# Two block inversions shared by columns between VectorE and GpSimd, with masks, roots, loads and value products placed anew

## The chip, the cores and the metric

The kernel runs on one core of a Trainium2 chip. The metric is the device time of one execution in microseconds. Before the change it was 1900.02 us, the median of three runs (1899.34 to 1905.55).

## What is computed

One step of a small hybrid network, with a model width of 1024, on 640 tokens: 128 of context and 512 of a latent grid with 64 columns and 8 rows. Layer 0 mixes tokens with a gated DeltaNet in both directions (8 heads of 128), layer 1 with attention over a neighbourhood of the grid and over all context keys (16 heads of 64). Each is followed by a gated feed-forward layer with a convolution of width 3. Cut to what matters here, for one direction of one head of the DeltaNet:

```
a_mat = jnp.where(strict, jnp.einsum('nbhid,nbhjd->nbhij', kb, kc) * decay, 0.0)
t_mat = lax.linalg.triangular_solve(eye + a_mat, eye, left_side=True, lower=True)
u = jnp.einsum('nbhij,nbhjd->nbhid', t_mat, vc * bc[..., None])
w = jnp.einsum('nbhij,nbhjd->nbhid', t_mat, kb * jnp.exp(gc)[..., None])
...
def step(s, inp):
    v_new = ui - jnp.einsum('bhcd,bhde->bhce', wi, s)
    o = (jnp.einsum('bhcd,bhde->bhce', qi * jnp.exp(gi)[..., None], s)
         + jnp.einsum('bhcj,bhje->bhce', intra, v_new))
    s = (s * jnp.exp(g_last)[..., None, None]
         + jnp.einsum('bhcd,bhce->bhde', ki * jnp.exp(g_last[..., None] - gi)[..., None], v_new))
...
o = rmsnorm(o, norm_g) * jax.nn.silu(z.reshape(B, T, GDN_HEADS, GDN_DV))
```

`decay` is the exponential of a masked difference of cumulated gates. The triangular solve is the inverse of a unit triangular matrix per chunk. In layer 1 the part that the change touches is the sum over values, over the neighbourhood and over the context:

```
return (jnp.einsum('bhqrk,brkhd->bqhd', p_loc, v_blk)
        + jnp.einsum('bhqc,bchd->bqhd', p_ctx, v_ctx))
```

## The kernel before, in words

Activations lie with the width on the partitions and the tokens as columns. A projection (`prod`, L385 to L387) is made of three products of parts, high by high, low by high and high by low; `weights` loads each weight tile and splits it on ACT (L373) and on VectorE or GpSimd (L375). The stages follow each other in the trace: the start to about 60 us, the eight DeltaNet heads to about 550, the output projection, the feed-forward layer 0 to about 1050, attention from about 1100 to 1395, the feed-forward layer 1 to the end.

The heads' stage is a list of steps, `SCHED` (L573), of which each is a letter and a head: k, q, v and z are projections with convolution, K (`decay` and `keys`) makes the decay mask `dec` and the matrix `M` with its transpose `MT`, and stores its 32 x 32 diagonal blocks (`md`) from SyncE's queue. I (`invert`) inverts the diagonal blocks of two heads at once, so there are four inversions, I0 to I3. M (`merge`) builds the inverse of each head's whole chunks from the inverted blocks by matmuls of 32 and 64 columns (L848 and behind). Q and V make query products and scaled values, S (`scan`) runs the recurrence in five steps a direction, F (`finish`) the norm and the gate, a is a part of the next layers' modulation. A scheduler orders each engine's instructions statically from the steps' priorities (`PR`: S 2000, M 500, K 200, I 100, the others none) and from their dependences. At run time each engine, and each DMA queue, takes its instructions in that order.

An inversion works on 80 lanes (2 heads, 4 blocks, 2 directions, 5 chunks), each a 32 x 32 block in one partition. `lN` is loaded by SyncE's queue (L806); 31 steps of a multiplication into `lP` (L813) and an addition into `lY` (L819) run on GpSimd; then `lY` is stored (`yd`, L820), transposed by a copy into `lN` (L821) and stored (`wd`, L822), both from GpSimd's queue. Each of the three tiles has one buffer, so that an inversion begins when the one before it has let go of them.

`merge` fetches the blocks: `W6` and `Wx` are the tiles of factors, `M` takes the diagonal blocks beside its other ones. The loads of `M` (L834, L835) stand ahead of those of `W6` and `Wx` (L836 to L841). The page writes W for W6. The first product, p1, is made of pieces of W6, Wx and M; copies on VectorE (L865 and behind) bring p2 back into `M`.

`decay` adds the columns on VectorE (L698), masks each direction with an `affine_select` on GpSimd (L703), and takes the exponential on ACT (L708). `finish` works out the scale `so` of the norm in five small operations of VectorE (L984 to L988) and a power on GpSimd (L989); VectorE then scales the outputs `osb` (L991) and PE transposes them (L994).

In attention, a block of 128 queries and a pair of heads takes six value matmuls: per head two over the neighbourhood (L1324) and one over the context (L1327). The two heads of a pair lie in two halves of the array's columns.

Of the kernel before, what the change touches and what calls it, by code (L numbers as in the profile page):

```python
# [13 lines left out]
F32R = mybir.dt.float32r  # L14
AF = mybir.ActivationFunctionType
# [19 lines left out]
PR = {"S": 2000, "I": 100, "M": 500, "K": 200}  # L35
# [544 lines left out]
class Gdn:  # L580
# [17 lines left out]
    def tokens(self):  # L598
# [4 lines left out]
        for t, sgn in ((self.UT, 1), (self.LT, -1)):  # L603
            nc.gpsimd.affine_select(
                out=t, in_=net.ones, pattern=[[sgn, 128]], compare_op=ALU.is_ge, fill=0.0, base=0,
                channel_multiplier=-sgn,
            )
        abT = self.gp.tile([128, W], F32, tag="kT", name="abT", bufs=4)
# [69 lines left out]
    def decay(self, h):  # L678


        nc = self.nc
        t = self.gp.tile([128, 2, NBLK, 128], F32, tag="dec", name=f"dec{h}", bufs=4)
        self.dec[h] = t
        ngc = self.ngc.rearrange("p b (d h) -> p d b h", d=2)[:, :, :, h]
        for n, (out, col, parts) in enumerate((
            (t[:, 0, 1:], ngc[:, 0, 1:], [(0, b) for b in range(1, NBLK)]),
            (t[:, 1, 1:], ngc[:, 1, 1:], [(1, b) for b in range(1, NBLK)]),
            (t[:, :, 0], ngc[:, :, 0], [(0, 0), (1, 0)]),
        )):
# [12 lines left out]
        for d, sgn in ((0, 1), (1, -1)):  # L702
            nc.gpsimd.affine_select(  # L703
                out=t[:, d], in_=t[:, d], pattern=[[0, NBLK], [sgn, 128]], compare_op=ALU.is_ge, fill=-1e30,
                base=0, channel_multiplier=-sgn,
            )
        f = t.rearrange("p d b i -> p (d b i)")
        nc.scalar.activation(f, f, AF.Exp)  # L708
# [90 lines left out]
    def invert(self, nh, md, yd, wd, name):  # L799
# [5 lines left out]
        P = self.gp.tile([128, 256], F32, tag="lP", name=f"lP{name}", bufs=1)  # L805
        nc.sync.dma_start(N[:L], md.rearrange("h q d b r c -> (h q d b) r c")[:L])  # L806
# [3 lines left out]
        for i in range(31, 0, -1):  # L810
            n = 32 - i
            pr = P[:L, : i * n].rearrange("p (j c) -> p j c", c=n)
            nc.gpsimd.tensor_tensor(  # L813
                pr,
                N[:L, :i, i : i + 1].to_broadcast([L, i, n]),
                Y[:L, i : i + 1, i:].to_broadcast([L, i, n]),
                ALU.mult,
            )
            nc.gpsimd.tensor_tensor(Y[:L, :i, i:], Y[:L, :i, i:], pr, ALU.add)  # L819
# [4 lines left out]
    def merge(self, h, yd, wd):  # L824
# [6 lines left out]
        v = lambda t, q, d: t[q, d].rearrange("b r c -> r b c")  # L831
        for q in range(4):
            s = slice(32 * q, 32 * q + 32)
            nc.sync.dma_start(M[s, 0, :, s], v(yd, q, 0))  # L834
            nc.sync.dma_start(M[s, 1, :, s], v(wd, q, 1))  # L835
        nc.sync.dma_start(W6[0:32, :, 0:32], v(wd, 0, 0))  # L836
        nc.sync.dma_start(W6[32:64, :, 32:64], v(wd, 1, 0))
        nc.sync.dma_start(W6[64:96, :, 0:32], v(yd, 2, 1))
        nc.sync.dma_start(W6[96:128, :, 32:64], v(yd, 3, 1))
        nc.sync.dma_start(Wx[64:96], v(wd, 2, 0))  # L840
        nc.sync.dma_start(Wx[32:64], v(yd, 1, 1))  # L841
# [134 lines left out]
    def finish(self, h):  # L976
# [4 lines left out]
        so = gp.tile([128, 4, NBLK], F32, tag="so", name=f"so{h}", bufs=2)  # L981
        for b in range(NBLK):
            nc.scalar.activation(sq[:, b], osb[:, b], AF.Square, accum_out=so[:, 0, b : b + 1])
        nc.vector.tensor_scalar(so[:, 1], ssq, 128.0, None, ALU.mult)  # L984
        nc.vector.reciprocal(so[:, 2], so[:, 1])
        nc.vector.tensor_tensor(so[:, 0], so[:, 0], so[:, 2], ALU.mult)
        nc.vector.tensor_scalar(so[:, 0], so[:, 0], 1.0 / 128, EPS, ALU.mult, ALU.add)
        nc.vector.tensor_tensor(so[:, 0], so[:, 0], so[:, 1], ALU.mult)  # L988
        nc.gpsimd.tensor_tensor(so[:, 3], so[:, 0], self.net.mhalf[:, :NBLK], ALU.pow)  # L989
# [33 lines left out]
    def run(self):  # L1023
# [4 lines left out]
        def step(op, h):  # L1028
# [14 lines left out]
            elif op == "I":  # L1043
                self.invert(2, *scr[h], h)
# [17 lines left out]
        for t in SCHED.split():  # L1062
            if t[0] in PR:
                with net.tc.high_priority(PR[t[0]]):
# [86 lines left out]
class Na:  # L1151
# [91 lines left out]
    def attend(self, p):  # L1243
# [51 lines left out]
        for cb in range(4):  # L1295
# [25 lines left out]
            for e in range(2):  # L1321
                out = O[H[e], cb * 128 : cb * 128 + 128]
                for j in range(2):
                    nc.tensor.matmul(  # L1324
                        out, vw[:n, cb, j, H[e]], pt[:n, 2 * e + j], start=(j == 0), stop=False, tile_position=(0, 64 * e)
                    )
                nc.tensor.matmul(  # L1327
                    out, self.cv[:, p * 128 + 64 * e : p * 128 + 64 * e + 64], pc[:, e], start=False, stop=True,
                    tile_position=(0, 64 * e),
                )  # L1330
# [313 lines left out]
```

## Time and profile before

| what | number |
|---|---|
| median of three runs | 1900.02 us |
| profiled execution | 1899.56 us |
| its span | 1897.9 us |
| granted clock of PE, mean | 0.977 |
| PEclk, 50 to 250 us and 350 to 400 us | 0.86 to 0.90 |
| inversions on GpSimd, first operation | 114.5, 188.1, 318.8, 431.9 us |

The profile is of one execution. Busy time is the time in which an engine ran an instruction; the span is from the first to the last. In lists of the trace a row has start, length, engine, line, operation, output and inputs, and in square brackets the idle time ahead of it and what ended it. A row of waits gives the total time, how often, and the longest. A line that a helper holds, such as L385, stands for many uses, told apart by the tiles' names, where numbers are left out.

### The profile page before, as it was taken

To read this page: it belongs to the slowest core of one execution; us is meant where nothing else is said; L and a number is where in the kernel's file an instruction comes from. 1 tells how busy PE (TensorE), PEld (TensorE's weight loads), DVE (VectorE), ACT (ScalarE), POOL (GpSimd) and SP (SyncE) were. 2 spreads that over 40 slices of the span, in tenths; PEclk is the share of its full clock that TensorE was granted. 3 is DMA by queue.
4 is the path that set the end of the run, shared out by engine and by line. 5 is a ranking of instruction groups with operands and counts; after the bars stand their busy time and mean duration, and the time that the engine had idled before them with its cause. 6 is when DMAs were issued, how large, how long until landed. Compare 5 with 4: busy or idle time off the path is not lost.

```text
span 1897.9 us, 34312 instructions
## 1 busy us (share of the span) xinstructions
PE 1794.2 (95%) x13587; PEld 1710.2 (90%) x13587; DVE 1207.2 (64%) x2876; ACT 725.2 (38%) x1458; POOL 345.5 (18%) x549
## 2 busy tenths in 40 slices
PE   6886699899999999999999999999999999999998
PEld 5885689799889999999999988888899999999998
DVE  6664467475567999755356699555678743553564
ACT  4444235254353331232234444444453421431443
POOL 1364703518002112100000211111131000000000
PEclk9897899899999999999999999999999999999999
DMA  7223133322242455442223254222233312222231
GB/s 294 73 83 84 36 114 107 92 79 81 63 150 69 161 173 159 140 156 62 87 86 104 76 163 154 78 70 69 69 123 119 121 53 77 87 71 76 88 91 56
DMA packets 102481, 194.16 MB, mean 102 GB/s; under 512 B 39496, under 2 KB 59034, under 8 KB 99560
## 3 DMA queue, kind: packets, MB, share of 16 engines
q1 hardware_dynamic: 93760, 162.88, 27.0%
q0 software_dynamic: 8016, 28.56, 4.7%
q8 instruction: 107, 1.75, 0.4%
q10 hardware_dynamic: 544, 0.52, 0.1%
q14 instruction: 54, 0.44, 0.1%
HBM read 183.09 MB, written 12.46 MB: 103 GB/s over the span
## 4 chain that ended last, share of the span: by engine, by line
PE 48%; DVE 5%; issue 2%; DMA 2%; ACT 1%; POOL 0%; DVEq 0%; POOLq 0%; ACTq 0%
PE duv L385 4%; PE duv L386 4%; PE duv L387 4%; PE dug L385 4%; PE dug L386 4%; PE dug L387 4%; PE rdn L385 4%; PE rdn L386 4%; PE rdn L387 4%; PE dvn L385 1%; DMA bias<-cols 1%; PE dvn L387 1%; PE dvn L386 1%; PE no L1324 1%; PE dqn L385 1%
## 5 line engine op out<-in xcount | busy, mean ns | idle before, releaser
L385 PE MATMUL duv<-hh,whuv 128*128 128x256 f32 (+1 forms) x704 | 217.6, 309 | 6.0 <-DVE yv L442 6.0
L385 PE MATMUL rdn<-F,whdn 128*128 128x384 f32 (+1 forms) x704 | 216.2, 307 | 2.5 <-DVE X L451 2.5
L387 PE MATMUL duv<-hh,wluv 128*128 128x256 f32 (+1 forms) x704 | 217.0, 308 | 0.4 <-DVE wluv L375 0.4
L386 PE MATMUL duv<-hl,whuv 128*128 128x256 f32 (+1 forms) x704 | 217.1, 308 | 0.0
L385 PE MATMUL dug<-hh,whug 128*128 128x256 f32 (+1 forms) x704 | 215.7, 306 | 1.0 <-DVE yg L442 1.0
L386 PE MATMUL dug<-hl,whug 128*128 128x256 f32 (+1 forms) x704 | 215.7, 306 | 0.0
L387 PE MATMUL dug<-hh,wlug 128*128 128x256 f32 (+1 forms) x704 | 215.7, 306 | 0.0
L386 PE MATMUL rdn<-F,whdn 128*128 128x384 f32 (+1 forms) x704 | 215.6, 306 | 0.0
L387 PE MATMUL rdn<-F,wldn 128*128 128x384 f32 (+1 forms) x704 | 215.5, 306 | 0.0
L385 PEld LDWEIGHTS duv<-hh,whuv 128*128 128x128 f32 x704 | 133.4, 189 | 6.6 <-ACT whug L373 3.8
L385 PEld LDWEIGHTS rdn<-F,whdn 128*128 128x128 f32 x704 | 132.4, 188 | 3.1 <-PE rdn L387 1.9
L387 PEld LDWEIGHTS duv<-hh,wluv 128*128 128x128 f32 x704 | 133.2, 189 | 0.8 <-DVE wluv L375 0.8
L385 PEld LDWEIGHTS dug<-hh,whug 128*128 128x128 f32 x704 | 132.5, 188 | 1.2 <-issue 1.2
L386 PEld LDWEIGHTS duv<-hl,whuv 128*128 128x128 f32 x704 | 133.2, 189 | 0.0
L386 PEld LDWEIGHTS rdn<-F,whdn 128*128 128x128 f32 x704 | 132.2, 188 | 0.0
L387 PEld LDWEIGHTS dug<-hh,wlug 128*128 128x128 f32 x704 | 132.2, 188 | 0.0
L387 PEld LDWEIGHTS rdn<-F,wldn 128*128 128x128 f32 x704 | 132.1, 188 | 0.0
L386 PEld LDWEIGHTS dug<-hl,whug 128*128 128x128 f32 x704 | 132.1, 188 | 0.0
L451 DVE SCALAR_TENSOR_TENSOR X<-rdn,mods,X 128x128 f32<-128x128 f32 (+1 forms) x144 | 54.9, 432 | 116.7 <-PE rdn L387 116.5
L373 ACT CAST whdn<-wstdn 128x896 fp32r<-128x896 f32 (+1 forms) x48 | 47.0, 979 | 211.5 <-PE rdn L386 120.9
L373 ACT CAST whug<-wstug 128x1024 fp32r<-128x1024 f32 x44 | 46.2, 1050 | 143.8 <-PE dug L386 120.4
L375 DVE TENSOR_TENSOR wldn<-wstdn,whdn 128x896 fp32r<-128x896 f32 (+1 forms) x48 | 54.3, 1132 | 58.9 <-ACT whdn L373 58.9
(704 smaller groups left out, 4823.7 us busy)
## 6 DMA issues: line engine op xcount, KB each, us to landing
wstuv<-w_up SPq DMA_DIRECT2D x44, 512.0 KB, 3.5
wstug<-w_up SPq DMA_DIRECT2D x44, 512.0 KB, 3.5
adat<-w_ada SPq DMA_DIRECT2D x20, 1024.0 KB, 6.7
adr<-w_adar POOLq DMA_DIRECT2D x80, 256.0 KB, 3.1
wstdn<-w_dn SPq DMA_DIRECT2D x32, 448.0 KB, 3.3
wstdn<-w_dn SPq DMA_DIRECT2D x16, 512.0 KB, 3.5
adr<-w_adar SPq DMA_DIRECT2D x32, 256.0 KB, 2.8
wstqT<-w_gin SPq DMA_DIRECT2D x8, 512.0 KB, 4.4
```

What stands on the lines that cost most here:

```text
L373: nc.scalar.copy(wh[:, c], st[:, c])
L375: ins = eng.tensor_tensor(wl[:, c], st[:, c], wh[:, c].bitcast(F32), ALU.subtract).ins
L385: nc.tensor.matmul(out, a, mh, start=first, stop=False)
L386: nc.tensor.matmul(out, a, ml, start=False, stop=False)
L387: ins = nc.tensor.matmul(out, b, mh, start=False, stop=last).ins
L451: nc.vector.scalar_tensor_tensor(x, ps[:, base + c0 : base + c1], self.mod(l, gi, m, v), x, ALU.mult, ALU.add)
L1324: nc.tensor.matmul(out, vw[:n, cb, j, H[e]], pt[:n, 2 * e + j], start=(j == 0), stop=False, tile_position=(0, 64 * e))
```

## The change

`invert` gets a column `cut`: columns from the cut on are worked by VectorE, those below it by GpSimd, with two parts of a wider `lP`. `CUT` is 24, 24, 32, 32, so that I0 and I1 give 8 of 32 columns to VectorE (62 operations; GpSimd keeps 46 of its 62), and I2 and I3 stay on GpSimd. I0's priority becomes 1000. The load of `lN` moves from SyncE's queue to GpSimd's. In `merge` four loads, two for W6 and two for Wx, stand first. The decay mask becomes an addition of a constant tile `far` (0 or -1e30), which GpSimd builds once; VectorE does the addition. The power in `finish` becomes an integer seed and three Newton steps on VectorE. The value matmuls alternate between the two heads.

```diff
-PR = {"S": 2000, "I": 100, "M": 500, "K": 200}
+CUT = (24, 24, 32, 32)
+PR = {"S": 2000, "I": 100, "I0": 1000, "M": 500, "K": 200}
...
+        self.far = self.gs.tile([128, 2, 128], F32, tag="far", name="far")
+        nc.gpsimd.memset(self.far, 0.0)
+        for d, sgn in ((0, 1), (1, -1)):
+            nc.gpsimd.affine_select(
+                out=self.far[:, d], in_=self.far[:, d], pattern=[[sgn, 128]], compare_op=ALU.is_ge, fill=-1e30,
+                base=0, channel_multiplier=-sgn,
+            )
...
-        for d, sgn in ((0, 1), (1, -1)):
-            nc.gpsimd.affine_select(
-                out=t[:, d], in_=t[:, d], pattern=[[0, NBLK], [sgn, 128]], compare_op=ALU.is_ge, fill=-1e30,
-                base=0, channel_multiplier=-sgn,
+        for d in range(2):
+            nc.vector.tensor_tensor(
+                t[:, d], t[:, d], self.far[:, d].unsqueeze(1).to_broadcast([128, NBLK, 128]), ALU.add
             )
...
-        P = self.gp.tile([128, 256], F32, tag="lP", name=f"lP{name}", bufs=1)
-        nc.sync.dma_start(N[:L], md.rearrange("h q d b r c -> (h q d b) r c")[:L])
+        P = self.gp.tile([128, 336], F32, tag="lP", name=f"lP{name}", bufs=1)
+        P = P[:, 144:], P
+        nc.gpsimd.dma_start(N[:L], md.rearrange("h q d b r c -> (h q d b) r c")[:L])
...
         for i in range(31, 0, -1):
-            n = 32 - i
-            pr = P[:L, : i * n].rearrange("p (j c) -> p j c", c=n)
-            nc.gpsimd.tensor_tensor(
-                pr,
-                N[:L, :i, i : i + 1].to_broadcast([L, i, n]),
-                Y[:L, i : i + 1, i:].to_broadcast([L, i, n]),
-                ALU.mult,
-            )
-            nc.gpsimd.tensor_tensor(Y[:L, :i, i:], Y[:L, :i, i:], pr, ALU.add)
+            for eng, p, lo, hi in ((nc.vector, P[0], max(i, cut), 32), (nc.gpsimd, P[1], i, cut)):
+                n = hi - lo
+                if n > 0:
+                    pr = p[:L, : i * n].rearrange("p (j c) -> p j c", c=n)
+                    eng.tensor_tensor(
+                        pr,
+                        N[:L, :i, i : i + 1].to_broadcast([L, i, n]),
+                        Y[:L, i : i + 1, lo:hi].to_broadcast([L, i, n]),
+                        ALU.mult,
+                    )
+                    eng.tensor_tensor(Y[:L, :i, lo:hi], Y[:L, :i, lo:hi], pr, ALU.add)
...
+        nc.sync.dma_start(W6[96:128, :, 32:64], v(yd, 3, 1))
+        nc.sync.dma_start(Wx[32:64], v(yd, 1, 1))
+        nc.sync.dma_start(W6[0:32, :, 0:32], v(wd, 0, 0))
+        nc.sync.dma_start(Wx[64:96], v(wd, 2, 0))
         for q in range(4):
...
-        nc.sync.dma_start(W6[0:32, :, 0:32], v(wd, 0, 0))
         nc.sync.dma_start(W6[32:64, :, 32:64], v(wd, 1, 0))
         nc.sync.dma_start(W6[64:96, :, 0:32], v(yd, 2, 1))
-        nc.sync.dma_start(W6[96:128, :, 32:64], v(yd, 3, 1))
-        nc.sync.dma_start(Wx[64:96], v(wd, 2, 0))
-        nc.sync.dma_start(Wx[32:64], v(yd, 1, 1))
...
-        nc.vector.tensor_scalar(so[:, 1], ssq, 128.0, None, ALU.mult)
-        nc.vector.reciprocal(so[:, 2], so[:, 1])
-        nc.vector.tensor_tensor(so[:, 0], so[:, 0], so[:, 2], ALU.mult)
-        nc.vector.tensor_scalar(so[:, 0], so[:, 0], 1.0 / 128, EPS, ALU.mult, ALU.add)
-        nc.vector.tensor_tensor(so[:, 0], so[:, 0], so[:, 1], ALU.mult)
-        nc.gpsimd.tensor_tensor(so[:, 3], so[:, 0], self.net.mhalf[:, :NBLK], ALU.pow)
+        V.tensor_scalar(so[:, 1], ssq, 128 * EPS, None, ALU.mult)
+        V.scalar_tensor_tensor(so[:, 0], so[:, 0], 1.0 / 128, so[:, 1], ALU.mult, ALU.add)
+        x, t, y = so[:, 0], so[:, 2], so[:, 3]
+        V.tensor_scalar(t.bitcast(I32), x.bitcast(I32), 1, None, ALU.logical_shift_right)
+        V.tensor_scalar(y.bitcast(I32), t.bitcast(I32), -1.0, float(0x5F3759DF), ALU.mult, ALU.add)
+        V.tensor_scalar(x, x, -0.5, None, ALU.mult)
+        for _ in range(3):
+            V.tensor_tensor(t, y, y, ALU.mult)
+            V.tensor_tensor(t, t, x, ALU.mult)
+            V.scalar_tensor_tensor(y, t, 1.5, y, ALU.add, ALU.mult)
...
-                self.invert(2, *scr[h], h)
+                self.invert(2, *scr[h], h, CUT[h])
...
-            for e in range(2):
-                out = O[H[e], cb * 128 : cb * 128 + 128]
-                for j in range(2):
+            for j in range(3):
+                for e in range(2):
```

The scheduler places the instructions anew. On GpSimd, in the middle of I0 (lP0, lN0 and lY0 are its tiles), stood head 3's two masks before; behind the additions stands the shape of a lane's part:

```order
L813 TENSOR_TENSOR lP0_1326<-lN0_1324,lY0_1325 80x231
L819 TENSOR_TENSOR lY0_1325<-lY0_1325,lP0_1326 80x11x21
L813 TENSOR_TENSOR lP0_1326<-lN0_1324,lY0_1325 80x220
L703 AFFINE_SELECT dec3_1244<-dec3_1244 128x640 x2
L819 TENSOR_TENSOR lY0_1325<-lY0_1325,lP0_1326 80x10x22
L813 TENSOR_TENSOR lP0_1326<-lN0_1324,lY0_1325 80x207
```

The same part of I0 on GpSimd now, with its smaller shapes:

```order
L831 TENSOR_TENSOR lY0_1317<-lY0_1317,lP0_1318 80x13x11
L825 TENSOR_TENSOR lP0_1318<-lN0_1316,lY0_1317 80x144
L831 TENSOR_TENSOR lY0_1317<-lY0_1317,lP0_1318 80x12x12
L781 TENSOR_TENSOR irk2_1053<-k2ss_1046,half_626 128x5
L825 TENSOR_TENSOR lP0_1318<-lN0_1316,lY0_1317 80x143
L831 TENSOR_TENSOR lY0_1317<-lY0_1317,lP0_1318 80x11x13
```

The masks dec3 are gone from the inversion, and so is the power of so0 from I1 further behind; the small operation irk2 of head 2's keys, which stood inside I0 before too, is still there.

On VectorE, at the copies that bring M0's product p2 back, the rows were these (dec0 and kq0s belong to head 0's queries, wlqT2 to a weight tile, vT2 to head 2's value projection):

```order
L898 TENSOR_TENSOR dec0_721<-kq0s_1425,dec0_721 128x512 x2
L375 TENSOR_TENSOR wlqT2_2533<-wstqT20_2530,whqT2_2532 128x1024
L865 COPY M0_780<-p20_1693 32x5x32 x4
L869 COPY W60_1652<-p30_1714 32x5x32 x2
L442 SCALAR_TENSOR_TENSOR vT2_1813<-dvT20_1763,sm_61,vT2_1813 128x127
L442 SCALAR_TENSOR_TENSOR vT2_1813<-dvT20_1763,sm_61,vT2_1813 128x254
```

Now the first nine operations of I1 (lP1, lN1, lY1) stand between the weight tile and M0's copies:

```order
L377 TENSOR_TENSOR wlqT2_2617<-wstqT20_2614,whqT2_2616 128x1024
L825 TENSOR_TENSOR lP1_1555<-lN1_1553,lY1_1554 80x31
L831 TENSOR_TENSOR lY1_1554<-lY1_1554,lP1_1555 80x31
L825 TENSOR_TENSOR lP1_1555<-lN1_1553,lY1_1554 80x60
L831 TENSOR_TENSOR lY1_1554<-lY1_1554,lP1_1555 80x30x2
L825 TENSOR_TENSOR lP1_1555<-lN1_1553,lY1_1554 80x87
L831 TENSOR_TENSOR lY1_1554<-lY1_1554,lP1_1555 80x29x3
L825 TENSOR_TENSOR lP1_1555<-lN1_1553,lY1_1554 80x112
L831 TENSOR_TENSOR lY1_1554<-lY1_1554,lP1_1555 80x28x4
L825 TENSOR_TENSOR lP1_1555<-lN1_1553,lY1_1554 80x135
L877 COPY M0_784<-p20_1777 32x5x32 x4
L881 COPY W60_1736<-p30_1798 32x5x32 x2
```

From there on operations of I1 stand singly between those of the scan S0 and of M0.

On PE, ahead of M0's first product p10, stood the last products of the second half of head 0's z projection (dzs01, from hh and hl, the two parts of the input):

```order
L385 MATMUL dzs01_2443<-hh_75,whzs0_2414 128x260
L386 MATMUL dzs01_2443<-hl_76,whzs0_2414 128x260
L742 MATMUL v0tp_1507<-ident_63,vT0_1492 128x128
L387 MATMUL dzs01_2443<-hh_75,wlzs0_2415 128x260
L848 MATMUL p10_1670<-W60_1652,M0_780 32x32
L848 MATMUL p10_1670<-Wx0_1653,M0_780 32x32 x2
```

Now 22 products of the first half of head 1's (dzs10) stand there, of which the last four are shown ahead of it, and p10 begins among them:

```order
L387 MATMUL dzs10_2561<-hh_75,whzs1_2557 128x384
L388 MATMUL dzs10_2561<-hl_76,whzs1_2557 128x384
L389 MATMUL dzs10_2561<-hh_75,wlzs1_2558 128x384
L387 MATMUL dzs10_2561<-hh_75,whzs1_2557 128x384
L860 MATMUL p10_1754<-W60_1736,M0_784 32x32
L388 MATMUL dzs10_2561<-hl_76,whzs1_2557 128x384
L389 MATMUL dzs10_2561<-hh_75,wlzs1_2558 128x384
```

So a part of one dense projection that came behind M0 stands ahead of it.

More of the change, by code (lines that the diff above doesn't have):

```diff
@@ L14 @@
 F32R = mybir.dt.float32r
+I32 = mybir.dt.int32
 AF = mybir.ActivationFunctionType
@@ L797, in keys, with invert @@
                 )
-    def invert(self, nh, md, yd, wd, name):
+    def invert(self, nh, md, yd, wd, name, cut=32):
         nc = self.nc
@@ L981, in finish @@
         so = gp.tile([128, 4, NBLK], F32, tag="so", name=f"so{h}", bufs=2)
+        V = nc.vector
         for b in range(NBLK):
             nc.scalar.activation(sq[:, b], osb[:, b], AF.Square, accum_out=so[:, 0, b : b + 1])
-        nc.vector.tensor_scalar(so[:, 1], ssq, 128.0, None, ALU.mult)
-        nc.vector.reciprocal(so[:, 2], so[:, 1])
-        nc.vector.tensor_tensor(so[:, 0], so[:, 0], so[:, 2], ALU.mult)
-        nc.vector.tensor_scalar(so[:, 0], so[:, 0], 1.0 / 128, EPS, ALU.mult, ALU.add)
-        nc.vector.tensor_tensor(so[:, 0], so[:, 0], so[:, 1], ALU.mult)
-        nc.gpsimd.tensor_tensor(so[:, 3], so[:, 0], self.net.mhalf[:, :NBLK], ALU.pow)
+        V.tensor_scalar(so[:, 1], ssq, 128 * EPS, None, ALU.mult)
[8 more added lines that the diff above has]
+            V.scalar_tensor_tensor(y, t, 1.5, y, ALU.add, ALU.mult)
         for b in range(NBLK):
@@ L1063, in run @@
             if t[0] in PR:
-                with net.tc.high_priority(PR[t[0]]):
+                with net.tc.high_priority(PR.get(t, PR[t[0]])):
                     step(t[0], int(t[1]))
@@ L1320, in attend @@
             yield
-            for e in range(2):
-                out = O[H[e], cb * 128 : cb * 128 + 128]
-                for j in range(2):
+            for j in range(3):
+                for e in range(2):
+                    if j < 2:
+                        v_, p_ = vw[:n, cb, j, H[e]], pt[:n, 2 * e + j]
+                    else:
+                        v_, p_ = self.cv[:, p * 128 + 64 * e : p * 128 + 64 * e + 64], pc[:, e]
                     nc.tensor.matmul(
-                        out, vw[:n, cb, j, H[e]], pt[:n, 2 * e + j], start=(j == 0), stop=False, tile_position=(0, 64 * e)
-                    )
[L1327 to L1330, printed above, removed]
+                        O[H[e], cb * 128 : cb * 128 + 128], v_, p_, start=(j == 0), stop=(j == 2),
+                        tile_position=(0, 64 * e),
+                    )
             ps = nxt
```

## The prediction

> **What bounds the kernel now.** The page comes first, for the engine that carries the span; then the waits of PE, for the places where PE stands still; then the waits of the other engines around the largest.
>
> ```profile
> span 1897.9 us, 34312 instructions
> PE 1794.2 (95%) x13587; PEld 1710.2 (90%) x13587; DVE 1207.2 (64%) x2876; ACT 725.2 (38%) x1458; POOL 345.5 (18%) x549
> ...
> PE kk3s L761 <- ACT k3ts L751: 16.7, 1, 16.7
> PE sb L925 <- ACT osb L957: 14.7, 1, 14.7
> ...
> PE p L848 <- DMA W<-wd: 9.4, 3, 5.1
> ...
> ACT dec L708 <- POOL dec L703: 16.9, 1, 16.9
> DVE osb L991 <- POOL so L989: 15.3, 1, 15.3
> ACT osb L957 <- DVE w L953: 19.0, 5, 15.7
> ```
>
> PE is busy 1794.2 of 1897.9 us, so 103.7 us of idle time is all that this change can win, apart from the values and from a slow clock. (The profiled execution took 1899.56 us: the span and 1.66 around it. The sum below is against it; it is 0.46 under the median.) The columns of the waits are total, times and longest. The two largest inside the work are single stalls, and the last three rows name their causes: ACT stood 16.9 us behind a decay mask that GpSimd had not done, and VectorE 15.3 us behind the power `so`. Both are GpSimd instructions, queued behind an inversion:
>
> ```profile
> 114.53 0.25 POOL L813 TENSOR_TENSOR lP<-lN,lY 80x31 f32<-80x31 f32 x1 [4.68 <-DMA lN<-md]
> 144.91 1.45 POOL L703 TENSOR_SCALAR_AFFINE_SELECT dec<-dec 128x640 f32<-128x640 f32 x2
> 156.75 0.25 POOL L819 TENSOR_TENSOR lY<-lY,lP 80x31 f32<-80x31 f32 x1
> ...
> 168.48 0.22 PE L848 MATMUL p<-W,M 32*32 32x32 f32 x2 [3.38 <-DMA W<-wd]
> 169.46 0.52 PE L848 MATMUL p<-Wx,M 32*32 32x32 f32 x3 [0.77 <-DMA Wx<-wd]
> ...
> 220.55 1.17 POOL L989 TENSOR_TENSOR so<-so,mhalf 128x5 f32<-128x5 f32 x1
> ```
>
> I0 runs from 114.53 to 157.0 with head 3's masks near its end, at 144.91. M0's first product comes at 168.48, 11.5 us after I0. So the 16.7 us stall and M0's 3.38 and 0.77 hang on one thing, I0's elapsed time: without the masks PE is at M0 earlier and waits there. The second stall ends with the power at 220.55, inside I1.
>
> **a) I0 in two halves, up to M0.** A GpSimd operation is priced by its smallest and largest shapes.
>
> ```profile
> 139.37 0.67 POOL L819 TENSOR_TENSOR lY<-lY,lP 80x252 f32<-80x252 f32 x1
> ...
> 118.20 1.21 DVE L375 TENSOR_TENSOR wlvT<-wstvT,whvT 128x1024 fp32r<-128x1024 f32 x1
> 119.34 0.43 DVE L780 TENSOR_SCALAR D<-D 128x5 f32<-128x5 f32 x1
> 119.69 0.15 DVE L781 TENSOR_TENSOR D<-D,edl 128x5 f32<-128x5 f32 x1
> 119.76 0.15 DVE L780 TENSOR_SCALAR D<-D 128x5 f32<-128x5 f32 x1
> L557 DVE TENSOR_TENSOR yv<-yv,yg 128x640 f32<-128x640 f32 x44 | 36.2, 823 | 25.4 <-ACT yg L556 25.4
> ```
>
> From 0.25 us (31 elements) to 0.67 (252) it is 1.9 ns an element over 0.19; the gap to the next is about 0.08. GpSimd keeps 46 of 62 operations and 4600 of 10,912 elements: 46 x 0.27 + 4600 x 0.0019 = 21.2, and 1.2 for the one power left among them (irk2, priced as the one of `so`): 22 us, done near 137. VectorE gets 62 operations, 6312 elements. It has no row of this shape; from 0.15 us (5), 0.82 (640) and 1.21 (1024) it is 1.04 ns an element, with starts 0.07 apart (119.69, 119.76): 62 x 0.07 + 6312 x 0.00104 = 10.9 us. These stand one by one among its other work:
>
> ```profile
> 109.00:157.00 48.00, 31.23 (x215) 29.85 (x213) 23.15 (x66) 17.68 (x36) 38.69 (x67) 0.82 0.23 67
> 180.00:201.00 21.00, 20.96 (x251) 18.55 (x249) 12.75 (x40) 8.60 (x33) 11.11 (x24) 1.00 0.42 132
> 201.00:225.00 24.00, 9.27 (x74) 8.17 (x73) 6.27 (x16) 6.65 (x25) 21.52 (x36) 0.77 0.08 28
> 225.00:240.00 15.00, 14.11 (x101) 13.20 (x100) 9.61 (x28) 4.72 (x11) 6.43 (x12) 0.92 0.30 69
> ```
>
> The columns are the window, its length, busy time of PE, PEld, DVE, ACT and POOL with counts, and the clock. DVE is busy 23.15 of the 48 us; some 21 of it falls behind 114.5. Packed, its half ends at 114.5 + 10.9 + 21 = 147 (an estimate). The other end comes from a contention that the rows show:
>
> ```profile
> 118.33 1.41 POOL L819 TENSOR_TENSOR lY<-lY,lP 80x135 f32<-80x135 f32 x1
> 153.38 0.46 POOL L819 TENSOR_TENSOR lY<-lY,lP 80x135 f32<-80x135 f32 x1
> ```
>
> The same add takes 0.46 us at 153.38 and 1.41 at 118.33, where VectorE's 128x1024 subtraction (118.20, 1.21 long) lies over it; and L780 behind that took 0.43 us instead of 0.15, until 119.77, as the add ended. So here either blocked the other for a whole operation. If no part of the split ran beside the other, and half of VectorE's other 21 us (taken as the part with two tiles of SBUF to read) did not either, the end is 114.5 + 22 + 10.9 + 10.5 = 158. I take the middle, 152.5: the blocking rows are those of long operations, and VectorE's half has short ones, but its queue also waits for PE.
>
> From I0's end to M0 lay 11.5 us. Of the loads that p1 (M0's first product) needs, some stood last:
>
> ```profile
> 160.44 0.55 POOL L822 DMA_DIRECT2D wd<-lN  x1 [0.31 <-POOL lN L821]
> ...
> 167.54 0.43 SPq L840 DMA_DIRECT2D Wx<-wd  x1
> ...
> lN<-md SPq DMA_DIRECT2D x4, 320.0 KB, 6.1
> ...
> wd<-lN POOLq DMA_DIRECT2D x4, 320.0 KB, 3.0
> ...
> 1112.83 0.34 PE L386 MATMUL dkn<-hl,whkn 128*128 128x384 f32 x1
> 1113.00 0.34 PE L387 MATMUL dkn<-hh,wlkn 128*128 128x384 f32 x1
> ```
>
> Wx's piece was issued at 167.54, after ten others; now it is among the first four, but it cannot start before `wd` has landed (issue 160.44, 3.0 us). Four issues of 0.43 to 0.5 us go from ahead of it: 1.9 us off, so 9.6. M0 is at 157 to 168, taken 162.1: -6.4. PE also does 22 products of head 1's z, 0.17 us apart (1112.83, 1113.00), 3.8 us, ahead of M0 that stood behind it; half of it I count as won, -2. **Together -8** (0 to -16: M0 at 168 with nothing won, or at 157 with all of it). PE itself could be at M0 at 168.5 - 3.4 - 16.7 + 3.8 = 152, so I0's end decides.
>
> **b) I1's VectorE half, among the scans.** In 180 to 201, S0 runs: PE is busy 20.96 of 21 us, so products fill the scan's waits, and DVE 12.75. An operation of I1's half is on average 0.15 + 6312/62 x 0.00104 = 0.26 us, 16 us for all; in DVE's 8.25 idle us they cost nothing, ahead of a scan operation all of it. I take a third exposed: +5 (0 to 16). Nine of them also stand ahead of M0's copies:
>
> ```profile
> 171.71 1.32 DVE L865 COPY M<-p 32x160 f32<-32x160 f32 x4 [5.26 <-PE p L848]
> ```
>
> They wait for lN's load, which is issued behind the `wd` store on GpSimd's queue: 160.44 - 157.0 + 0.3 and 3.0 us for the store, 6.1 for the load (3.0 if it lands like the store), 2.5 for the nine: 15.3 us after I0's end, or 12.2. The copies came 3.2 us behind M0's first product, so now 9.6 + 3.2 = 12.8 after I0. So +2 (0 to 2.5). **Together +7.**
>
> **c) The power gone from I1.** The 14.7 us stall goes: `so` is worked out on VectorE in 14 operations of 0.15 to 0.2 us, 2.5 us in place of a wait of 15.3. The clock stood at 0.92 for 14.11 busy us behind the stall: 1.1 more. **-16** (-10 if the merge M2 is next late: of the 9.4 us in three waits for W it has 0.9, beside 5.1 and 3.4).
>
> **d) M4, behind I2, which stays on GpSimd whole.**
>
> ```profile
> 318.78 0.25 POOL L813 TENSOR_TENSOR lP<-lN,lY 80x31 f32<-80x31 f32 x1 [2.63 <-DMA lN<-md]
> 356.82 1.11 POOL L819 TENSOR_TENSOR lY<-lY,lP 80x31 f32<-80x31 f32 x1
> 368.41 0.28 PE L848 MATMUL p<-W,M 32*32 32x32 f32 x2 [5.10 <-DMA W<-wd]
> ```
>
> PE waits 5.1 us there. Between head 5's key products and M4 the order has products that take 50 us at full clock before and 39 now (each at the spacing of its shape; an estimate), so PE is there 11 us earlier in the chain. The chain gets some 4.5 us shorter (1.9 for the reordered loads, up to 3.1 for a load that lands like a store on GpSimd's queue). 11 - 4.5, less 1.5 as the moved products fill gaps ahead of M2: **+5** (-2 with a tie between the two, +9 with a chain no shorter).
>
> **e) Attention values,** 32 blocks:
>
> ```profile
> 1113.27 0.71 PE L1324 MATMUL no<-ptw,vw 92*64 92x128 f32 x6
> 1113.76 0.28 PE L1327 MATMUL no<-ptc,cv 128*64 128x128 f32 x1
> 1113.81 0.27 PE L1324 MATMUL no<-ptw,vw 92*64 92x128 f32 x1
> 1114.03 0.38 PE L1327 MATMUL no<-ptc,cv 128*64 128x128 f32 x2
> ```
>
> Where both column halves run (1113.76 to 1113.92), starts are 0.055 us apart; alone, twice that. The twelve start over 0.87 us (to 1114.14); in turn 11 x 0.055 = 0.60. 0.25 x 32 = **-8** (0 to -9).
>
> **f) Masks and root on VectorE:** 16 adds of 128x640 x 0.82 = 13 us, and 8 roots of 2.5 us; DVE is idle 36% and each takes the place of a trip to GpSimd: **0** (-2 to +2). Uncovered, the 13 us would come in full.
>
> Sum: -8 + 7 - 16 + 5 - 8 + 0 = -20, so 1879.6, **1880 us**.
>
> **Rivals.** *R1, blocking at every step.* M0 comes at 168 (a = -2), and each exposed operation waits for GpSimd's too (b = +12): -2 + 12 - 16 + 5 - 8 = -9, 1890. For it: 118.33 and 119.34. Against: these operations are 0.26 us, the subtraction 1.21. The Trainium skill, "SBUF — State Buffer", section "🔬 SBUF: two separate sides", says the same: VectorE with two SBUF inputs and GpSimd share a port pair as an exclusive lock, held for the whole instruction, and the loser blocks. By it 1890; the trace agrees for the long subtraction, and no run yet shows it for short ones.
>
> *R2, the scans stretch (slower).* VectorE is in order. If an I1 operation, its own 0.26 us and 0.4 of waiting, stands in the scan's chain, 62 x 0.66 = 41 us. Without b the sum is -27, so the gain is gone from 25 / 62 = 0.40 us exposed per operation (with 2 ahead of M0). At 85% exposed, +35 + 2: 1910. For it: one operation stands between nearly every two of the scan. Against: PE has products to fill, 20.96 of 21.
>
> *R3, little contention:* I0's end at 147, b and d at 0: -16 - 16 - 8 = -40, 1860.
>
> *R4, the value order does nothing,* since PE already overlaps as far as it can: +8, 1888. For it: half of the twelve overlap now.
>
> **How the numbers follow.** Forecast 0.45 (1870 to 1889), R1 0.20, R3 0.17, R4 0.10, R2 0.08. A measurement tells 0.3%, 5.7 us, from no change. Faster by more than that (under 1894) are the forecast, R3, R4 and half of R1: 0.82; the other half of R1 is the same, 0.10; R2 slower, 0.08. The range leaves out R2 and the far half of R3: 1858 to 1898.
>
> **What would show it.** The stalls at kk3s and before sb gone, M0's first product at 157 to 168 with a wait of some 10 us ahead of it, a longer wait at M4, twelve value starts over 0.6 us. GpSimd rows in I0 with twins of very unequal length would show R1; S0 over 26 us instead of 21, with PE idle in it, R2. The forecast is wrong if M2 or M4 waits over 15 us, or if VectorE's half of I0 ends behind 160.

## The result, and the profile after

The changed kernel took 1871.15 us, the median of four runs (1864.63 to 1878.59), against 1899.68 us before (the median of four runs now, 1899.20 to 1905.55): a ratio of 0.9845, with a 95% interval from 0.9821 to 0.9868. Run again, beside the experiments, it took 1874.67 us (1867.36 to 1877.04) against 1897.06, a ratio of 0.9877 [0.9857, 0.9897]. So it is 22 to 29 us faster. The profiled execution took 1866.71 us, 32.9 less than the one of before; both kernels vary by some 10 us from run to run, so that the traces show where the time went, and the medians how much it is. Two executions below, one of 2875.53 us without the split and one of 7543.15 us with the values by head, ran at a granted clock of 0.557 and 0.226 and are left out of every number.

The page's first lines after the change, and the largest waits of PE within the work (total, times, longest):

```profile
span 1864.9 us, 34461 instructions
PE 1781.6 (96%) x13587; PEld 1696.2 (91%) x13587; DVE 1257.2 (67%) x3088; ACT 725.4 (39%) x1458; POOL 299.4 (16%) x500
...
PE p L860 <- DMA W<-wd: 13.9, 2, 12.7
PE adp L186 <- DMA adat<-w_ada: 12.4, 1, 12.4
...
PE kk3p L769 <- ACT k3tp L759: 3.0, 1, 3.0
```

PE's idle time fell from 103.7 to 83.3 us, and its busy time by 12.6. The stalls of 16.7 and 14.7 us are gone; one of 12.7 us, at M4, is left, where 5.1 and 1.5 were. GpSimd's rows tell how the two inversions now run (start, length, operation, and in brackets what ended the idle time before):

```profile
115.73 0.23 POOL L825 TENSOR_TENSOR lP<-lN,lY 80x23 f32<-80x23 f32 x1 [2.98 <-DMA lN<-md]
118.75 1.71 POOL L825 TENSOR_TENSOR lP<-lN,lY 80x95 f32<-80x95 f32 x1
133.48 2.11 POOL L831 TENSOR_TENSOR lY<-lY,lP 80x128 f32<-80x128 f32 x1
142.46 0.27 POOL L831 TENSOR_TENSOR lY<-lY,lP 80x23 f32<-80x23 f32 x1
152.08 0.62 POOL L832 DMA_DIRECT2D yd<-lY  x1 [8.21 <-DVE lY L831]
158.20 0.51 POOL L816 DMA_DIRECT2D lN<-md  x1 [1.47 <-DMA M<-yd]
162.17 0.24 POOL L825 TENSOR_TENSOR lP<-lN,lY 80x23 f32<-80x23 f32 x1 [3.46 <-DMA lN<-md]
184.69 0.23 POOL L831 TENSOR_TENSOR lY<-lY,lP 80x23 f32<-80x23 f32 x1
215.41 0.56 POOL L832 DMA_DIRECT2D yd<-lY  x1 [22.71 <-DVE lY L831]
```

In both inversions GpSimd is done first and waits for VectorE, 8.2 us in I0 and 22.7 us in I1. I0 ends near 151.5 instead of 157.0. I1 starts at 162.2 instead of 188.1, and ends near 214.9 instead of 227.6, so it lasts longer than before and is done earlier. On PE, at M0 and M4:

```profile
162.28 0.24 PE L860 MATMUL p<-W,M 32*32 32x32 f32 x2 [1.16 <-DMA W<-wd]
350.40 0.28 PE L860 MATMUL p<-W,M 32*32 32x32 f32 x2 [12.70 <-DMA W<-wd]
```

And the same stretches of the heads as before (window, length, busy time of PE, PEld, DVE, ACT, POOL, then the clock):

```profile
180.00:201.00 21.00, 21.00 (x266) 18.86 (x265) 18.02 (x67) 9.32 (x33) 4.50 (x14) 1.00 0.05 14
201.00:225.00 24.00, 23.90 (x172) 22.74 (x170) 21.94 (x84) 10.59 (x30) 5.01 (x5) 1.00 0.31 85
225.00:240.00 15.00, 15.00 (x220) 12.34 (x220) 7.96 (x20) 4.62 (x10) 0.45 (x2) 1.00 0.42 104
```

From 201 to 225 us PE is busy 23.90 us instead of 9.27, at full clock instead of 0.77. VectorE is nearly full there, 21.94 of 24, and PE loses nothing by it.

The experiments ran on three chips, on which the kernel before took 1897.06, 1899.02 and 1899.05 us, so that ratios are compared where two runs were on different chips. The table gives two numbers of each profiled execution: the heads' time, from the start of the gate's product `gcp` to the first product `duv` of the feed-forward layer 0 (the varying start of the kernel is left out), and PE's idle time within it. The ratio of the times, to the kernel before on the same chip, stands beside them.

| kernel | heads, us | PE idle in them, us | ratio, 95% interval |
|---|---|---|---|
| before | 529.1 | 54.3 | 1 |
| changed | 502.5 | 31.5 | 0.9845 [0.9821, 0.9868] |
| changed, again | 506.2 | 30.5 | 0.9877 [0.9857, 0.9897] |
| no split | 527.3 | 53.7 | 0.9993 [0.9979, 1.0007] |
| no split, K3 early | 529.2 | 52.2 | 0.9985 [0.9969, 1.0002] |
| split of I0 alone | 512.7 | 37.4 | 0.9899 [0.9883, 0.9915] |
| roots on GpSimd | 514.9 | 33.7 | 0.9896 [0.9882, 0.9911] |
| masks on GpSimd | 512.7 | 37.3 | 0.9890 [0.9864, 0.9916] |
| both on GpSimd | 519.6 | 44.8 | 0.9926 [0.9905, 0.9946] |
| lN's load on SyncE | 512.5 | 35.1 | 0.9882 [0.9862, 0.9902] |
| old load order | 509.0 | 34.5 | 0.9875 [0.9846, 0.9903] |
| split of I0, I1, I2 | 508.6 | 27.5 | 0.9866 [0.9851, 0.9882] |
| split of all four | 508.9 | 29.4 | 0.9880 [0.9863, 0.9897] |
| values by head | 503.9 | 29.5 | 0.9890 [0.9870, 0.9909] |

Heads less idle, PE's busy time, is 471 to 481 us in every row. PE has the same products in all of them; busy time multiplied by the granted clock comes to 458 to 463 us (467 with all four split), and the other 10 to 20 us are what the lower clock took. So the change moves the idle time, and a difference of some 5 us between two single profiles can be the clock's.

### The profile page after: what moved, and what is told of

The parts are those of the page before. It is cut to its first block, busy times and chain, and to the rows that moved or that the text cites. A ratio compares the mean times of both kernels' runs of the same rounds, so it can differ in the third digit from the quotient of the medians.

```text
span 1864.9 us, 34461 instructions
## 1 busy us (share of the span) xinstructions
PE 1781.6 (96%) x13587; PEld 1696.2 (91%) x13587; DVE 1257.2 (67%) x3088; ACT 725.4 (39%) x1458; POOL 299.4 (16%) x500
## 4 chain that ended last, share of the span: by engine, by line
PE 71%; issue 10%; DVE 9%; DMA 4%; POOL 3%; ACT 2%; SPq 1%; POOLq 0%; DVEq 0%; ACTq 0%
PE duv L387 5%; PE duv L389 5%; PE duv L388 4%; PE dug L387 4%; PE dug L388 4%; PE dug L389 4%; PE rdn L387 4%; PE rdn L388 4%; PE rdn L389 4%; POOL adr L234 1%; PE p L860 1%; PE adp L186 1%; PE rgo L387 1%; PE rgo L388 1%; PE rgo L389 1%
```

## The experiments

**The changed kernel again** has no edit.

> The changed kernel once more, as the yardstick for the runs beside it. Its four times so far lie in two pairs, 1864.6 and 1866.7, 1875.6 and 1878.6. If the spread is of the kernel, both pairs show again (clock 0.982 and 0.978); if it was of that chip, all lie within 4 us. Ratio to the kernel before 0.982 to 0.988 either way.

Its five times were 1867.4, 1868.7, 1874.7, 1876.0 and 1877.0 us. The spread is the kernel's; differences of 4 us between two medians below are not told apart from it.

**No split.**

```diff
-CUT = (24, 24, 32, 32)
+CUT = (32, 32, 32, 32)
```

> The change without the split: I0 and I1 whole on GpSimd, all else as changed. Theory A (I0's elapsed time sets when M0 starts): I0 takes its 40 us and some 4 us of blocking, so M0's first product comes at about 170 instead of 162.3, and the total is 6 to 9 us above the changed kernel. Rival B (the gain of the heads came from masks and roots leaving GpSimd's queue, the split itself gives nothing, since VectorE's queue is full): M0's first product within 2 us of 162.3, total within 3 us of the changed kernel.

It is as slow as before, 1897.19 against 1897.06 us, and 22.5 us above the changed kernel: neither theory expected that. The waits name it (PE's waits, then its two rows, then the load of I1 on GpSimd's queue):

```profile
PE p L860 <- DMA W<-wd: 40.9, 3, 20.1
...
167.32 0.28 PE L860 MATMUL p<-W,M 32*32 32x32 f32 x2 [20.09 <-DMA W<-wd]
236.82 0.31 PE L860 MATMUL p<-W,M 32*32 32x32 f32 x2 [16.28 <-DMA W<-wd]
...
182.52 0.51 POOL L816 DMA_DIRECT2D lN<-md  x1 [5.66 <-DMA md<-MT]
```

Before, PE had waited 16.7 us at kk3s and 3.4 at M0, together 20.1; now it waits 20.1 at M0. Before, it had waited 14.7 us for the finish and 0.9 at M2, together 15.6; now 16.3 at M2. Masks and power had been only the first instructions to show a wait whose length the inversion set. (The alternated values are in this run too, and its attention is 6 us shorter than before, as in the other runs that have them; but the stretch behind the last value product, which the change leaves alone, took 521.5 us instead of 518.1, and over all runs it takes 516 to 522.)

**Split of I0 alone.**

```diff
-CUT = (24, 24, 32, 32)
+CUT = (24, 32, 32, 32)
```

> Only I0 is split, I1 is whole on GpSimd again. Theory A (I1's operations on VectorE cost nothing, PE has products to fill the scans; I1 is not on the path as M2 has over 10 us to spare): total within 3 us of the changed kernel, scans S0 and S1 each within 1.5 us of 21.9 and 21.2. Rival B (they cost the 7 us of the prediction, hidden by a gain elsewhere): total 4 to 8 us below the changed kernel, S0 back to 20.8 us or less. Rival C (I1's shorter time is worth something): M2 waits, total 3 us or more above.

1878.53 us. I1, whole on GpSimd, starts at 160.0 and is stored at 198.8:

```profile
156.16 0.51 POOL L816 DMA_DIRECT2D lN<-md  x1 [0.95 <-DMA Wx<-yd]
...
198.77 0.56 POOL L832 DMA_DIRECT2D yd<-lY  x1 [0.29 <-POOL lY L831]
...
PE p L860 <- DMA W<-wd: 20.8, 3, 15.5
```

That is 16.6 us earlier than in the changed kernel, whose VectorE half holds it. So the split of I1 makes I1 later. Yet M2 waits 15.5 us here and not there: without I1's split M2's first product is number 1379 of PE's products in the trace, with it number 1574, behind more dense work. The 15.5 us are not all lost: M4 waits 4.1 us here and 12.7 in the changed kernel. The total is 4 us above the changed kernel run beside it, at the edge of what can be told apart. So rival C's two numbers come out, M2's wait and 3 us or more, but not for its reason, since I1 is not longer but shorter and earlier here. The split of I0 alone gives 19 of the 22 us. I1 can start so early because of the stores that its load waits for: with I0 split, head 3's (`md`) were issued from 142.8 us on (145.0 in the changed kernel), ahead of M0's loads on SyncE's queue; without it, from 175.2 on, behind them.

**Values by head**, with the two loops exchanged as before.

```diff
-            for j in range(3):
-                for e in range(2):
+            for e in range(2):
+                for j in range(3):
```

> Only the order of the value products goes back: one head's three, then the other's. Theory A (two column halves run beside each other): attention longer by 6.5 us, from 260.0 to 266.5 us between the first and the last value product, total 5 to 8 us above the changed kernel. Rival B (attention's shorter time comes from what the heads left behind, such as a better clock): no more than 1 us.

From first to last value product it took 266.1 us, against 266.5 before, 260.0 in the changed kernel and 260.9 in its second profile; in all twelve traces with alternated values it is 259.2 to 261.2. Theory A is borne out in the trace, at some 6 us. The total does not show it: the median of the three executions, 1875.47 us, is 0.8 us above the changed kernel run beside it, which is within the spread.

**Roots on GpSimd, and masks on GpSimd**, each alone.

```diff
-        V.tensor_scalar(so[:, 1], ssq, 128 * EPS, None, ALU.mult)
...
-            V.scalar_tensor_tensor(y, t, 1.5, y, ALU.add, ALU.mult)
+        nc.vector.tensor_scalar(so[:, 1], ssq, 128.0, None, ALU.mult)
...
+        nc.gpsimd.tensor_tensor(so[:, 3], so[:, 0], self.net.mhalf[:, :NBLK], ALU.pow)
```

> The changed kernel with the roots of the finish back on GpSimd as a power. The run without the split waited 16.3 us at M2 although the power was gone. Theory A (the stall of 14.7 us was I1's elapsed time, named after whichever instruction stood behind it): with I1 split, GpSimd is free from 185 us on, the power of head 0 runs when it is asked, no stall above 3 us between 180 and 235, total within 3 us of the changed kernel. Rival B (the power's trip to GpSimd cost it, as the prediction's part c has it): a stall of 8 us or more in front of sb or osb returns, total 8 us or more above.

```diff
-            nc.vector.tensor_tensor(
-                t[:, d], t[:, d], self.far[:, d].unsqueeze(1).to_broadcast([128, NBLK, 128]), ALU.add
-            )
+            nc.gpsimd.affine_select(
+                out=t[:, d], in_=t[:, d], pattern=[[0, NBLK], [sgn, 128]], compare_op=ALU.is_ge, fill=-1e30,
+                base=0, channel_multiplier=-sgn,
+            )
```

> The changed kernel with the decay masks back on GpSimd; head 3's stand behind the last operation of GpSimd's half of I0. Theory A (a mask behind the inversion holds ACT, head 3's key products and the VectorE operations that stand among I0's other half): ACT waits some 8 to 10 us for the mask, M0's first product comes 5 to 10 us later, total 4 to 10 us above the changed kernel. Rival B (M0 waits for I0 anyway, so the mask's place is of no weight): total within 3 us.

With the roots on GpSimd no stall of over 3 us stands between 180 and 235 us, as theory A has it. But the heads are 8.7 to 12.4 us longer, behind 340 us; the powers of heads 3 and 4 stand ahead of and inside I3 there, which is still whole on GpSimd (its row, and VectorE's and PE's waits from 370 to 475 us):

```profile
423.53 1.19 POOL L1002 TENSOR_TENSOR so<-so,mhalf 128x5 f32<-128x5 f32 x1
...
DVE osb L1004 <- POOL so L1002: 7.2, 3, 4.5
...
PE q5ts L748 <- DVE M L896: 3.5, 1, 3.5
```

Only a part of it is idle time (33.7 against 30.5 to 31.5); the rest is slower PE time, in an execution where the clock was 0.70 from 340 to 380 us (0.79 in the changed kernel). By the ratios the kernel is 4 to 10 us above the changed kernel's two measurements (the median is 1878.49 us); how much of that is the roots stays open.

With the masks on GpSimd, head 3's stand behind the last operation of I0's half, at 140.1 us, and PE waits 7.1 us for the key products that need ACT:

```profile
140.09 1.45 POOL L712 TENSOR_SCALAR_AFFINE_SELECT dec<-dec 128x640 f32<-128x640 f32 x2
...
PE kk3p L770 <- ACT k3tp L760: 7.1, 1, 7.1
```

ACT waited 7.4 us for the mask, and M0's first product came at 167.5 instead of 162.3; theory A holds in the trace, with 6 to 10 us in the heads. By the ratios the total (1877.08 us) is 2 to 9 us above the changed kernel's, and its interval overlaps theirs.

**Split of I0, I1 and I2, and of all four.**

```diff
-CUT = (24, 24, 32, 32)
+CUT = (24, 24, 24, 32)
```

> I2 is split as well, at column 24. In the changed kernel M4 waits 12.7 to 13.3 us for it. Theory A (I2's elapsed time sets M4): its 39 us become 27 to 31, M4's wait falls to 5 us or less, total 5 to 9 us below the changed kernel. Rival B (VectorE's operations lie in the scans S2 and S3, whose products PE then lacks): M4's wait falls, but the scans from 300 to 350 us get longer by as much, total within 2 us. Rival C: M4 is then held by its other inputs, 2 to 4 us below.

```diff
-CUT = (24, 24, 32, 32)
+CUT = (24, 24, 24, 24)
```

> I3 is split too. In the changed kernel no wait for M6's loads above 1.5 us is seen, so I3's time is not on the path. Theory A: total within 2 us of the kernel with I0 to I2 split. Rival B (62 operations more on VectorE stretch S4 and S5): 3 to 6 us above that one. Rival C (products that stand ahead of M6 move up and fill gaps elsewhere): 3 us or more below it.

M4's wait goes: PE's waits for W total 6.0 us in three, the longest, 4.0, now at M6. The time does not go down: 1873.2 and 1874.05 us, as the changed kernel. From 340 to 530 us the first of the two, then the changed kernel's second profile:

```profile
340.00:370.00 30.00, 28.56 (x297) 26.00 (x292) 16.58 (x57) 9.41 (x21) 4.85 (x6) 1.00 0.34 94
370.00:460.00 90.00, 83.94 (x738) 75.33 (x738) 68.55 (x212) 43.66 (x136) 40.40 (x71) 0.96 0.23 71
460.00:530.00 70.00, 62.17 (x638) 55.82 (x637) 48.00 (x163) 32.83 (x116) 1.36 (x4) 0.91 0.28 86
```

```profile
340.00:370.00 30.00, 16.64 (x203) 13.72 (x202) 10.96 (x23) 5.16 (x12) 9.07 (x20) 0.72 0.34 85
370.00:460.00 90.00, 87.39 (x765) 80.85 (x763) 72.33 (x221) 45.06 (x129) 41.68 (x70) 1.00 0.27 79
460.00:530.00 70.00, 65.72 (x680) 59.73 (x681) 46.28 (x152) 35.41 (x126) 1.01 (x3) 0.98 0.28 86
```

M4's stretch has 11.9 us less idle time, the two behind it 3.5 and 3.6 us more, and their clock is 0.96 and 0.91 instead of 1.00 and 0.98. That is near rival B's total (by the ratios 2 us below and 4 above the changed kernel's two), in another place than it named: not S2 and S3, but the stretches behind them. Splitting I3 too changes nothing that can be told apart, theory A of that run.

**lN's load on SyncE's queue.**

```diff
-        nc.gpsimd.dma_start(N[:L], md.rearrange("h q d b r c -> (h q d b) r c")[:L])
+        nc.sync.dma_start(N[:L], md.rearrange("h q d b r c -> (h q d b) r c")[:L])
```

> The changed kernel with lN's load back on SyncE's queue, where I1's stands behind M1's loads; I1's first VectorE operations are then placed behind M0's copies. Theory A (when I1 starts counts): lN1 is issued near 172 instead of 158 us, I1 ends 8 to 14 us later, M2 waits, total 3 to 10 us above the changed kernel. Rival B (I1 has room, M2's order adapts): total within 3 us.

I1's load was issued at 173.0 us, and I1's VectorE half ended at 227.8 instead of 214.9, as theory A has it. But M2 waited only 1.1 us, since the order had put more products ahead of it. 1876.1 us, by the ratios 1 to 7 us above the changed kernel: not decided.

**Masks and roots both on GpSimd**, the two edits above together.

> The split with masks and roots both back on GpSimd, that is the split with its load order and queue alone. Theory A (the split is the gain, the masks' and roots' places each cost some us, as in the two runs before, and add up): from the gate's product gcp to the first product of the feed-forward layer 12 to 18 us more than the changed kernel's 502.5 to 506.2, total 8 to 15 us above it, still some 8 us below the kernel before. Rival B (they are worth something only together): total at the kernel before's, over 20 us above. Rival C (one hides the other): no more than either alone, total 2 to 6 us above.

1885.22 us, a ratio of 0.9926, clear of the changed kernel, by 9 to 15 us, and of the kernel before, by 14. The heads took 519.6 us, 13 to 17 more: theory A, the two nearly add up.

**Merge loads in the old order**, with the four loads moved back behind the others.

> The changed kernel with the merge loads in their old order. Theory A: Wx's piece of wd is issued near 162 instead of 159.2, M0's first product comes 2 to 3 us later, total 1 to 4 us above the changed kernel. Rival B (PE is the bound at M0 since it waits only 1.2 us there): total within 1 us.

M0's first product came at 161.9 us, although Wx's piece of `wd` was issued at 161.1 instead of 159.2. 1876.06 us (1866.71 to 1881.33), and in the profiled execution 1866.71. That fits rival B. The heads are 3 to 6 us longer than the changed kernel's, with a wait of 14.5 us at M4, but no cost of the old order can be told apart in the time.

**No split, with K3 early.**

```diff
-CUT = (24, 24, 32, 32)
-PR = {"S": 2000, "I": 100, "I0": 1000, "M": 500, "K": 200}
+CUT = (32, 32, 32, 32)
+PR = {"S": 2000, "I": 100, "I0": 1000, "M": 500, "K": 200, "K3": 3000}
```

> No split, as in the run above, but head 3's keys (K3) with priority 3000, so that its blocks' stores stand among M0's loads on SyncE's queue and not behind M1's. In the run without the split I1's load waited for them until 182.5; here it is issued near 168. Theory A (a good part of the change's gain came from I1's earlier start, which the split brought about through the order): I1 ends near 214 instead of 228.3, M2's first product at 222 to 227 instead of 236.8, total 5 to 12 us below the run without the split. Rival B (the split itself carries the gain): total within 3 us of that run.

I1 ended at 214.9, and M2 came 12.7 us earlier, both as theory A expected:

```profile
224.12 0.28 PE L860 MATMUL p<-W,M 32*32 32x32 f32 x2 [14.43 <-DMA W<-wd]
```

The total is 1895.11 us, by the ratios 1.5 us below the run without the split: rival B. An earlier I1 is worth nothing as long as the order gives PE nothing to do while it runs: M0's 20.4 and M2's 14.4 us of waiting are still there, and M4's first product comes at 374.1 us, as in the run without the split (374.0).

## Why the prediction was right, and where it was not

The time, 1871.15 us, lies in the range (1858 to 1898) and 9 us under the 1880 forecast (the second median, 1874.67, 5 us); against the own time of the profile of before, the sum was -20 and the profile shows -32.9. By parts:

**a) M0** came at 162.28 us; 162.1 was forecast. I0 ended at 151.5 (152.5). GpSimd's half took 27 us, not 22, the VectorE half 36. That M0 came out to 0.2 us is partly luck, since I0 ended 1.0 us earlier and the way from there to M0 was 1.2 longer, 10.8 instead of 9.6. The wait of some 10 us ahead of M0 was 1.2. PE had just the 22 products more there that were counted, but came to M0 at 161, not at 152: in their place stand smaller waits, of which the largest are 3.0 us at kk3p (head 3's key products) for ACT, 1.3 for VectorE's qT and 0.9 for its M, and the 22 products added 5.4 us of busy time, not 3.8. From `gcp` to M0 PE's idle time fell from 21.0 to 8.9 us. So the -8 was -12: M0 is 6.7 us nearer to `gcp`, and the moved products are worth their 5.4 in full and not by half. Against the run without the split, where M0 comes 5 us later, waits 20 us and has 35 products fewer ahead of it, the moved products are the larger part, 9.2 us of busy time.

**b) I1's half among the scans** was mis-sized: +7 was forecast. From its first to its last product S0 took 21.9 us instead of 20.8 (20.9 with I1 whole on GpSimd), and M0's copies came 3.3 us behind M0's first product, as before 3.2:

```profile
162.12 0.20 DVE L825 TENSOR_TENSOR lP<-lN,lY 80x31 f32<-80x31 f32 x1 [2.63 <-DMA lN<-md]
...
165.55 1.32 DVE L877 COPY M<-p 32x160 f32<-32x160 f32 x4 [0.38 <-PE p L860]
```

The nine operations waited for lN1, which landed 10.5 us after I0's end, not 12.2 to 15.3, and were done before p2. The term is about +1: PE was busy throughout, as it was in 180 to 201 us before, and the third of 62 operations that the sum had exposed was not.

**c) The power.** The stall is gone, and the -16 was about the size of it: between the first products of M0 and of M2 PE's idle time fell from 17.0 to 0.9 us. Its reason was wrong, and the right size is luck. The step "The 14.7 us stall goes" rested on the power. Without the split the power is gone as well and M2 waits 16.3 us in its place; neither the -16 nor the fallback of -10, "if the merge M2 is next late", came there. An earlier I1 is not enough either, as PE's products in the traces show:

| kernel | I1 ends, us | products from M0's first to M2's first | PE idle between them, us |
|---|---|---|---|
| before | 227.6 | 569 | 17.0 |
| no split | 228.3 | 548 | 19.3 |
| no split, K3 early | 214.9 | 464 | 15.5 |
| split of I0 alone | 198.5 | 465 | 15.7 |
| changed | 214.9 | 660 | 0.9 |
| lN's load on SyncE | 227.8 | 734 | 1.2 |

With lN's load on SyncE's queue I1 ends as late as before and PE does not wait; with the split of I0 alone it ends 29 us earlier than before and PE waits. In these six it is the order that decides, by how much work it puts ahead of M2. What is ahead of M2 is then missing ahead of M4, which is part of d. The clock gave more than the 1.1 us counted: it was 1.00 over the whole of 165 to 240 us, and 0.86 before.

**d) M4** waits 12.7 us instead of 6.6, +6.1 where +5 was forecast. From head 5's key products to M4 it is 60.7 us instead of 65.3, 4.6 less (4.5). The run with I2 split shows that the time does not fall when this wait is removed.

**e) The values** gave 6.5 us of the 8. The twelve start within 0.61 us (0.60 was worked out):

```profile
1086.98 0.66 PE L1345 MATMUL no<-ptw,vw 92*64 92x128 f32 x8
1087.46 0.39 PE L1345 MATMUL no<-ptc,cv 128*64 128x128 f32 x4
```

**f) Masks and roots** were put at 0, for their work on VectorE. No run shows that work alone, since each that takes it off VectorE puts it into GpSimd's queue. Their absence from GpSimd's queue is worth something, but only with the split: together 13 to 17 us in the heads (from the run with both back), and without it, taken with the load order and lN's queue, about 2 (527.3 against 529.1).

Heads -12 were forecast (a to d) and -23 to -27 measured. Some 6 us of the difference are b and 4 are a; the first profile has 4 more because PE's busy time is shorter (471.1 instead of 474.8 us), which the second (475.7) does not have. The mechanism was wrong in one point: a and c were counted as two stalls with a cause each, a mask and a power, while the run without the split shows one thing behind both, the idle time of PE while an inversion runs. In the heads PE's idle time went from 54.3 to about 31 us: 12 less up to M0, 16 less from there to M2, 7 more from there to M4, and 1 to 3 less behind it. How much of this is I0's shorter time, and how much the order that the scheduler makes of it, stays open: the order was not held fixed by hand with and without the split.

**The rivals.** R1, blocking at every step: blocking occurs, and costs little. The row of 1.71 us at 118.75 (its like took 0.35 to 0.39) lies beside VectorE's subtraction of 1.21 us, the one of 2.11 at 133.48 beside the two mask additions that the change brought, and one of 1.36 at 140.34 (its like took 0.26) beside another subtraction. These three are 4 of the 5 us by which GpSimd's half of I0 was longer than 22; that of I1 took 22.8. All VectorE operations of the two inversions, in the groups of 110 to 220 us:

```profile
L825 DVE TENSOR_TENSOR lP<-lN,lY 80x112 f32<-80x112 f32 (+29 forms) x62 | 18.8, 303 | 3.9 <-DMA lN<-md 3.4
L831 DVE TENSOR_TENSOR lY<-lY,lP 80x112 f32<-80x112 f32 (+29 forms) x62 | 18.3, 295 | 0.4
```

That is 37.1 us for 124 operations, 18.6 an inversion, against 15.9 reckoned unblocked. The excess lies in the 73 that ran beside one of GpSimd's inversion operations: 26.4 us against 20.9 reckoned, 0.08 us each. The other 51 took 10.7, where 10.9 are reckoned. The lock that the Trainium skill describes ("SBUF — State Buffer", section "🔬 SBUF: two separate sides") agrees with the long rows; with short operations on both engines blocking took at most 2.7 us an inversion, and R1's M0 at 168 did not come. R2 did not occur: S0 grew by 1 us. R3's b, nothing, was near the measured +1; its 1860 was too low, since I0 ended at 151.5 and M4's wait grew. R4 is refuted by the values' rows.

## What to carry to other kernels

A wait is named after the instruction that ended it, but where that stood in an ordered queue behind something long, its length is that of the long thing: take the named instruction out of the queue and the wait can show up at the next one that needs the long thing, here with nearly the same length (20.1 and 16.3 us for 20.1 and 15.6). On a kernel whose bound engine is 95% busy, ask first which work it is given while a long side job runs: here a side job that ended 13 us earlier brought nothing while the order left PE without work, and removing the largest wait left brought nothing. Edits that are worth nothing alone (masks and roots here) can be worth some 10 us once the job that they stood behind has become short.

## What the runs showed of the hardware that was not expected

After the idle 12.7 us at M4 PE did not come back at full speed. In the changed kernel's profile the windows behind it show:

```profile
351.00:356.00 5.00, 4.99 (x103) 3.88 (x91) 2.72 (x6) 1.28 (x3) 0.00 (x0) 0.50 0.34 66
356.00:361.00 5.00, 5.00 (x47) 4.06 (x43) 3.04 (x6) 1.35 (x4) 0.45 (x2) 0.80 0.20 30
```

The granted clock was 0.50 for 5 us and 0.80 for the next five, so that the wait cost 3.5 us of full-speed time beyond its own length. In the kernel with I2 split, where no such wait is left at M4, the same followed a shorter one: behind the wait of 4.0 us at M6, which ends at 465.26, the clock was 0.51 from 465.5 to 472.5 us, then 1.00 for the next 51.
